# Small parts of weights: GpSimd's subtraction replaced by a negated copy on ScalarE and an accumulating DMA

## The chip, the cores and the metric

One core of a Trainium2 chip runs the program. The metric is the time of one execution in device microseconds (us). Engines are named as in the profile: PE (TensorE's products) and PEld (its weight loads), DVE (VectorE), ACT (ScalarE), POOL (GpSimd), SP (SyncE, which issues the loads).

## The reference

256 tokens of width 1024 go through two models one after the other, each of two layers and a final norm, in fp32. In a layer of the first ("block 1"):

```python
h = rmsnorm(x, norm_g)
proj = h @ w_in                       # split into 15 parts of four groups
y_a = conformer_conv(a_u, a_v, ...)   # 31 taps along the tokens, layernorm, silu
y_b = short_gated_conv(b_b, b_c, b_x, conv_b_w)
y_c = window_gqa(c_q, c_k, c_v, swa_sink)
y_d = neighborhood_attn(d_q, d_k, d_v, na_rpb)
x = x + concat([y_a*silu(a_z), y_b*silu(b_z), y_c*silu(c_z), y_d*silu(d_z)]) @ w_out
```

In a layer of the second ("block 2"):

```python
x = x + 0.5 * (silu(h @ wg) * (h @ wu)) @ wd   # ffn1, D_FF = 2816
x = x + mixing(rmsnorm(x))                     # forgetting and dilated attention, gated recurrence
x = x + 0.5 * (silu(h @ wg) * (h @ wu)) @ wd   # ffn2
```

## The kernel before

**Precision.** TensorE's fast format (fp32r) keeps fewer bits than fp32. So every weight w and every activation is split: hi = w rounded to fp32r, lo = w - hi. A product is made of three: hi by hi, hi by lo and lo by hi (`MM3`, `MMW`, `MM3n`).

**The weight stream.** All weights come from DRAM once, as 206 chunks in the order of their use, nearly all [128, 2048] fp32 (1 MB, sixteen 128x128 blocks). `weight_loads` asks for a tile `st` (3 buffers of them) and issues the load on SP. `weight_splits` takes chunk after chunk: it asks for a tile `hi` and a tile `lo` (3 buffers each) and works in halves [128, 1024]. For each half ACT copies st into hi, rounding, and then lo = st - hi is made on DVE or, for a share of the halves, on POOL: `share` is added up in `owed`, and each time it reaches 1 the half goes to POOL (`way = self.G`). The share is 0.6 in block 1 (`SHARE_A`), 0.25 in the feed-forward (`SHARE_F`) and 0.45 in the mixing of block 2 (`SHARE_B`); the first three chunks (`FAST`) never use POOL. After the last half st is free for the next load. `take` hands a chunk to the products, `drop` frees its hi and lo.

**Stages.** Two layers of block 1 (`mix_a`; the 31 taps of its convolution are 62 DVE instructions on the tile `ca`, from `hp`, in `a_u`); then twice feed-forward (`ffn`), mixing, feed-forward. In `ffn` the gate's sums leave the banks by `fg`, the up projection's by `fh`; `fs` is the gate after silu, `ha` the hidden operand.

**Order.** Each stage is a set of tasks (generators). `Scheduler.step` picks the instruction that can start first by its own estimates, less a priority; nothing but the order of instructions on each engine follows from them, and the waits are put in for the data. All helpers record their instructions at one line per kind: L470 is every ACT instruction, L493 every DVE and POOL one, L585 every DMA on SP, L574, L575 and L577 the products of `MMW`, L561 to L563 those of `MM3`.

Of the kernel before, what the change touches and what calls it, by code (L numbers as in the profile page):

```python
# [9 lines left out]
F32 = mybir.dt.float32  # L10
# [3 lines left out]
AF = mybir.ActivationFunctionType  # L14
# [4 lines left out]
T = 256  # L19
# [28 lines left out]
def out_order(nk, late):  # L48
    """(feature tile, k) of an output projection; the first tiles take the late k in a second sweep."""
    if not late:  # L50
        return [(fo, i) for fo in range(KT) for i in range(nk)]
    return ([(fo, i) for fo in range(OPEN) for i in range(nk - late)] +
            [(fo, i) for fo in range(OPEN) for i in range(nk - late, nk)] +
            [(fo, i) for fo in range(OPEN, KT) for i in range(nk)])
# [19 lines left out]
def weight_plan():  # L74
    """Chunks of the weight stream in the order of use: (key, source, layer, blocks);
    a block is (rows, columns) and lands as [128, len(columns)]."""
# [51 lines left out]
def const_arrays():  # L128
    """Tables that depend on the shapes alone."""
# [36 lines left out]
def param_columns(g):  # L166
    """Small parameters, features on partitions (layout only)."""
# [9 lines left out]
    for n in ("conv_a_w", "conv_b_w"):  # L177
# [26 lines left out]
FAST = 3  # L204
PARTS = {0: 4, 1: 4}
PRIO = dict(w1=0.8, w2=-1.8, w3=0.4, epilogue=0.5, gate=1.7, up=1.5, rstd=2.0, norm=1.3, values=0.7,
            conv=0.3, att=1.8, evac=1.1, level=0.3, prep=-0.7, rec=2.3, bias=-1.3, vg=0.2)
SHARE_F = 0.25
# [5 lines left out]
class Op:  # L214
    __slots__ = ("ways", "outs", "ins", "tset", "dep", "gen")

    def __init__(self, ways, outs, ins, tset=None):
        self.ways, self.outs, self.ins, self.tset = ways, outs, ins, tset
# [37 lines left out]
class Scheduler:  # L256
    """Orders the instructions of concurrent tasks (generators) by the estimated time at which each could start.
    Only the order follows from the estimates; every wait that the data needs is Tile's."""
# [20 lines left out]
    def advance(self, t):  # L279
        """Runs a task up to its next instruction, or until it has to wait."""  # L280
# [63 lines left out]
    def step(self):  # L344
# [41 lines left out]
        self.commit(op, eng, end)  # L386
# [11 lines left out]
class Builder:  # L398
# [104 lines left out]
    def VG(self, meth, out, *ins, **kw):  # L503
        """On the vector engine or, when that is done sooner, on GpSimd."""
        w, i = self._v("V", meth, out, ins, kw)
        w2, _ = self._v("G", meth, out, ins, kw)
        return Op([w, w2], [extent(out)], i)
# [28 lines left out]
    def MMs(self, products):  # L536
        """Products on distinct parts of the array, in one go: (out, lhsT, rhs, start, stop) each."""
# [16 lines left out]
    def MM3(self, out, ah, al, bh, bl, first, last):  # L554
        """Product of operands given as sums of two parts, less the product of the small parts."""
# [11 lines left out]
    def MMW(self, bank, wh, wl, x, first, last):  # L567
        """wh and wl against the parts x: [128, 2, 256], the bank's halves being the parts of the result."""
# [18 lines left out]

    def split(self, hi, lo, src):
# [21 lines left out]
    def weight_splits(self):  # L610
        for i in range(len(self.plan)):
# [5 lines left out]
            for j in range(parts):  # L617
# [5 lines left out]
                way = self.G if on_pool and i >= FAST else self.V  # L623
                yield way("tensor_tensor", lo[:, s], st[:, s], hi[:, s].bitcast(F32), op=ALU.subtract)
# [11 lines left out]
    def take(self, key):  # L636
        """The parts of the next chunk, its tiles, and the events of its pieces."""
# [12 lines left out]
    def dense_t(self, key, act, ready=None):  # L650
        """Features on partitions: a bank [128, nf, 256]."""
# [15 lines left out]
    def dense_w(self, key, act, ready):  # L667
        """Features on partitions: per feature tile a bank with the two parts of the result."""
# [13 lines left out]
    def dense_n(self, keys, act, width, ready=None):  # L682
        """Tokens on partitions: two banks, or halves of one, [128, width]."""
# [37 lines left out]
    def out_proj(self, key, act, nk, korder, late, coef, st, ready):  # L721
        """x += coef * act @ w, and the next norm's operands as the feature tiles finish."""
# [40 lines left out]
    def pair(self):  # L763
        """Operands of a product: large parts, small parts, and both side by side, [128, 8, 2, 256]."""
# [6 lines left out]
    def prep(self, st, fo):  # L771
        """x*g in two parts and the sums of squares, for feature tile fo."""
# [26 lines left out]
    def token_cols(self, tiles, out):  # L799
        """Sums over the partitions of [128, 256] tiles: [128 tokens, 2] in PSUM."""  # L800
# [10 lines left out]
    def bcast_cols(self, r, out):  # L811
        """[128 tokens, 2] to [128, 256] in PSUM, the same row on every partition."""
# [7 lines left out]
    def rstd(self, st, use):  # L820
        """st["r"]: [128 tokens, 2]; st["rbc"]: the same as rows, [128, 256], and what the phase asks for."""
# [131 lines left out]
    def heads(self, f, qT, kT, v, bias, nkeys, done, sink=None):  # L953
        """Heads 2f, 2f+1 (halves of feature tile f): qT(half, t), kT(half, n), v(kt, half), bias(half, t);
        done(bank) takes the bank with the outputs [128 (half, d), 256 queries]."""
# [62 lines left out]
    def rope(self, bank, ps, nf, cos, sin, o, tags):  # L1018
        """Rotary embedding of [128, nf, 256] with features on partitions, whose pairs lie 32 apart; o may hold the
        result."""  # L1020
# [14 lines left out]
    def mix_a(self, l, st, nxt):  # L1035
        nc, tc, s = self.nc, self.tc, self.s
        done = Event()
        with tc.tile_pool(name="mixa", bufs=1, reuse_waits="tile") as mp:
# [54 lines left out]
            def a_v(bank, ps):  # L1093
                """Raw like a_u: the norm's factor is applied here, to both."""
# [190 lines left out]
    def block_b_consts(self):  # L1285
        """Angles of the partial rotary embedding and the columns of the lower bounds."""
# [13 lines left out]
        # the angle over 2 pi modulo 1 with exact products: the angle in halves of 12 bits, 1 / 2 pi in three parts  # L1300
# [48 lines left out]
        # L = ln(max(lb, 1e-30)) in two steps that stay in the table's range  # L1349
# [11 lines left out]
    def mix_b(self, l, st, nxt):  # L1361
        nc, tc, s = self.nc, self.tc, self.s
        done = Event()
        with tc.tile_pool(name="mixb", bufs=1, reuse_waits="tile") as mp:
# [29 lines left out]
            def log1p_exp(ps, nch, cols=None):  # L1394
                """ln(1 + exp(-|z|)) for z and, given columns, for z + column."""
# [48 lines left out]
            def mixed(tl, m):  # L1444
                """Left halves of blocks of 2m from slot 0, right halves from slot 1."""
# [6 lines left out]
            def blocks(bank, t, left, right):  # L1452
                """left^T right within blocks of 64 tokens: [128 (block, s), (t, head), 64]."""
# [49 lines left out]
            def recurrence():  # L1503
                """A^T[s, t] of the gated recurrence: the diagonal, then pairs that meet in blocks of 2m tokens."""
# [120 lines left out]
            def dilated(f):  # L1625
                """One softmax over the keys of the three patterns, each key with its multiplicity."""
# [70 lines left out]
    def start(self, st):  # L1697
        """Loads, constants and the first norm's operands."""
# [35 lines left out]
    def warm(self):  # L1734
        """Keeps the tensor engine busy until the first operands are there, so that its clock is up by then."""
# [14 lines left out]
    def rescale(self, st, gf):  # L1750
        """x becomes the first block's output."""
# [136 lines left out]
```

## Time and profile before

| what | value |
|---|---|
| time, median of 3 runs | 1400.74 us (1397.69 to 1403.88) |
| profiled execution: span | 1401.3 us |
| PE busy | 1296.3 us (93%) |
| PEld busy | 1154.8 us (82%) |
| DVE busy | 1009.0 us (72%) |
| ACT busy | 776.4 us (55%) |
| POOL busy | 556.5 us (40%) |
| moved by DMA | 220.40 MB, 157 GB/s |

The page gives the profiled execution's time by its span alone; it is 0.6 us above the median. A busy share is a mean over stages that differ: what an engine's time is worth is read from the stage and from which wait ends last there. Busy times of PE are modelled.

### The profile page before, as it was taken

The page shows a single profiled execution, that of the slowest core. Times are in us where ns is not written, and L with a number is a line of the kernel's source. Part 1 is how long each engine was busy: PE and PEld are TensorE (multiplying, and loading weights), DVE is VectorE, ACT ScalarE, POOL GpSimd, SP SyncE. Part 2 cuts the span into 40 slices and gives each one's busy share as a digit, 9 for nine tenths or more (in the row PEclk, how much of TensorE's full clock was granted, in tenths as well). Part 3 has the DMA queues.
Part 4 walks back from the last instruction along what each step waited for, and adds up shares of the span by engine and source line. Part 5 has one row for each costly group of instructions (what it writes and reads, how often), then busy time and mean ns, then how long its engine had stood idle before and what let it go on. Part 6 is the DMA issues. An engine that isn't in the chain of part 4 may idle for free.

```text
span 1401.3 us, 21738 instructions
## 1 busy us (share of the span) xinstructions
PE 1296.3 (93%) x8530; PEld 1154.8 (82%) x8530; DVE 1009.0 (72%) x1478; ACT 776.4 (55%) x1277; POOL 556.5 (40%) x321
## 2 busy tenths in 40 slices
PE   8688996798989999889999999999999889999997
PEld 7677895787878789878788888888889778788886
DVE  7996789867997656778677656777656777677742
ACT  5444555355457547567555544556447667555542
POOL 5533662445324333553433323333333652433321
PEclk9888998899999999899999999999999989999999
DMA  7532543333536554323454554554554323455550
GB/s 261 188 120 72 156 157 120 120 121 120 185 122 213 202 185 151 132 80 121 158 200 183 188 203 155 204 182 181 192 191 156 126 83 127 151 182 196 193 181 31
DMA packets 39335, 220.40 MB, mean 157 GB/s; under 512 B 10176, under 2 KB 11968, under 8 KB 13760
## 3 DMA queue, kind: packets, MB, share of 16 engines
q1 hardware_dynamic: 39232, 219.01, 43.9%
q8 instruction: 67, 1.10, 0.3%
q14 instruction: 36, 0.29, 0.1%
HBM read 217.94 MB, written 1.05 MB: 156 GB/s over the span
## 4 chain that ended last, share of the span: by engine, by line
PE 62%; DVE 24%; ACT 6%; issue 5%; POOL 2%; DMA 0%; SPq 0%; DVEq 0%; POOLq 0%; ACTq 0%
PE bank L574 27%; PE bank L575 15%; DVE ca L493 6%; DVE lo L493 4%; PE bank L561 3%; PE bank L562 3%; PE bank L563 3%; PE bank L577 3%; DVE sp L493 3%; ACT hi L470 2%; PE bank L544 2%; DVE act L493 2%; PE bank L533 2%; DVE fh L493 2%; DVE x L493 1%
## 5 line engine op out<-in xcount | busy, mean ns | idle before, releaser
L493 POOL TENSOR_TENSOR lo<-st,hi 128x1024 fp32r<-128x1024 f32 (+1 forms) x142 | 354.5, 2499 | 483.4 <-ACT hi L470 481.2
L574 PE MATMUL bank<-act,hi 128*128 128x512 f32 x1456 | 524.5, 397 | 2.4 <-DVE act L493 2.3
L470 ACT ACTIVATE hi<-st 128x1024 fp32r<-128x1024 f32 (+3 forms) x416 | 428.2, 1035 | 90.3 <-PE bank L574 48.7
L575 PE MATMUL bank<-act,lo 128*128 128x256 f32 x1664 | 437.2, 283 | 5.0 <-DVE lo L493 4.2
L493 DVE TENSOR_TENSOR lo<-st,hi 128x1024 fp32r<-128x1024 f32 (+1 forms) x274 | 358.5, 1311 | 78.7 <-ACT hi L470 75.8
L575 PEld LDWEIGHTS bank<-act,lo 128*128 128x128 f32 x1664 | 315.6, 190 | 26.0 <-DVE lo L493 6.4
L574 PEld LDWEIGHTS bank<-act,hi 128*128 128x128 f32 x1456 | 276.2, 190 | 57.4 <-DVE act L493 3.6
L574 PE MATMUL bank<-ha,hi 128*128 128x512 f32 x672 | 238.1, 396 | 3.5 <-DVE ha L493 2.8
L561 PE MATMUL bank<-act,hi 128*128 128x256 f32 x720 | 214.7, 298 | 0.0
L562 PE MATMUL bank<-act,hi 128*128 128x256 f32 x720 | 205.7, 286 | 0.6 <-DVE act L493 0.6
L563 PE MATMUL bank<-act,lo 128*128 128x256 f32 x720 | 205.5, 285 | 0.0
L575 PE MATMUL bank<-ha,lo 128*128 128x256 f32 x704 | 193.3, 282 | 0.0
L574 PEld LDWEIGHTS bank<-ha,hi 128*128 128x128 f32 x672 | 126.8, 189 | 31.2 <-DVE ha L493 3.1
L561 PEld LDWEIGHTS bank<-act,hi 128*128 128x128 f32 x720 | 140.1, 195 | 6.4 <-issue 4.2
L562 PEld LDWEIGHTS bank<-act,hi 128*128 128x128 f32 x720 | 139.6, 194 | 1.1 <-DVE act L493 0.8
L563 PEld LDWEIGHTS bank<-act,lo 128*128 128x128 f32 x720 | 139.1, 193 | 0.0
L575 PEld LDWEIGHTS bank<-ha,lo 128*128 128x128 f32 x704 | 133.1, 189 | 2.8
L493 POOL TENSOR_TENSOR fs<-fs,rbc 128x512 f32<-128x512 f32 x44 | 62.0, 1410 | 114.5 <-ACT fs L470 108.0
L493 DVE SCALAR_TENSOR_TENSOR x<-bank,x 128x256 f32<-128x256 f32 x128 | 53.1, 420 | 68.7 <-PE bank L577 67.1
L493 POOL TENSOR_TENSOR sqa<-sqa,sq 128x256 f32<-128x256 f32 x60 | 54.1, 906 | 108.8 <-ACT sq L470 106.3
L577 PE MATMUL bank<-act,hi 128*128 128x512 f32 x208 | 83.1, 400 | 1.7 <-DVE act L493 1.7
L493 DVE SCALAR_TENSOR_TENSOR ca<-hp,cw,ca 128x256 f32<-128x256 f32 x120 | 81.1, 735 | 0.0
(218 smaller groups left out, 1601.4 us busy)
## 6 DMA issues: line engine op xcount, KB each, us to landing
st<-ws SPq DMA_DIRECT2D x197, 1024.0 KB, 4.8
st<-ws SPq DMA_DIRECT2D x2, 1040.0 KB, 4.8
st<-ws SPq DMA_DIRECT2D x4, 512.0 KB, 4.3
st<-ws SPq DMA_DIRECT2D x8, 192.0 KB, 5.2
nb<-rpb SPq DMA_DIRECT2D x16, 96.0 KB, 4.8
st<-ws SPq DMA_DIRECT2D x2, 768.0 KB, 4.3
out<-st SPq DMA_DIRECT2D x4, 256.0 KB, 2.8
cst<-cst SPq DMA_DIRECT2D x1, 832.5 KB, 8.7
```

Of the source, the lines that this page charges most:

```text
L470: return Op([("A", dur, lambda: self.nc.scalar.activation(out, in_, func, **kw))], outs, ins, ACT_SETS.get(func))
L493: return (eng, dur, lambda: fn(out, *ins, **kw)), [extent(a) for a in aps]
L533: return Op([("P", dur, lambda: self.nc.tensor.matmul(out, lhsT, rhs, start=start, stop=stop))], [extent(out)], [extent(lhsT), extent(rhs)])
L544: mm(o, l, r, start=st, stop=sp)
L561: mm(out, ah, bh, start=first, stop=False)
L562: mm(out, ah, bl, start=False, stop=False)
L563: mm(out, al, bh, start=False, stop=last)
L574: mm(out, wh, x, start=first, stop=False)
L575: mm(out[:, 0], wl, x[:, 0], start=False, stop=False)
L577: mm(out, wh, x, start=False, stop=True)
```

## The change

A half that fell to POOL is now made in two steps. ACT writes lo = -hi (a copy with scale -1), and then POOL issues a DMA that adds st to lo in place (`DMAadd`). POOL itself no longer works on the data. Which halves these are is decided by the same rule. The planner counts 1.2 us of POOL for an issue (`ADD_ISSUE`) and takes the result to be there 4.0 us later (`ADD_LATE`). Everything else of the diff removes comments.

```diff
+ADD_ISSUE = 1.2
+ADD_LATE = 4.0
...
-    def __init__(self, ways, outs, ins, tset=None):
-        self.ways, self.outs, self.ins, self.tset = ways, outs, ins, tset
+    def __init__(self, ways, outs, ins, tset=None, late=0.0):
+        self.ways, self.outs, self.ins, self.tset, self.late = ways, outs, ins, tset, late
...
-        self.commit(op, eng, end)
+        self.commit(op, eng, end + op.late)
...
+    def DMAadd(self, out, src):
+
+        return Op([("G", ADD_ISSUE, lambda: self.nc.gpsimd.dma_start(out, src, accum_op=ALU.add))],
+                  [extent(out)], [extent(src), extent(out)], late=ADD_LATE)
...
-                way = self.G if on_pool and i >= FAST else self.V
-                yield way("tensor_tensor", lo[:, s], st[:, s], hi[:, s].bitcast(F32), op=ALU.subtract)
+                if on_pool and i >= FAST:
+                    yield self.A(lo[:, s], hi[:, s].bitcast(F32), AF.Copy, scale=-1.0)
+                    yield self.DMAadd(lo[:, s].bitcast(F32), st[:, s])
+                else:
+                    yield self.tt(lo[:, s], st[:, s], hi[:, s].bitcast(F32), ALU.subtract)
```

There are 142 such halves before and 142 after. Since the planner's estimates change, it also orders other instructions differently.

**POOL in the first convolution.** lo_77, lo_78 and lo_79 are the three lo buffers. Before:

```order
L493 TENSOR_TENSOR lo_78<-st_73,hi_75 128x512
L493 TENSOR_TENSOR g_70<-par 128x8
L493 TENSOR_TENSOR lo_79<-st_71,hi_76 128x1024 x2
L493 TENSOR_TENSOR lo_77<-st_72,hi_74 128x1024
L493 TENSOR_TENSOR lo_78<-st_73,hi_75 128x1024
L493 TENSOR_TENSOR lo_79<-st_71,hi_76 128x1024
L493 TENSOR_TENSOR y_164<-oc,gz_162 128x256
L493 TENSOR_TENSOR lo_77<-st_72,hi_74 128x1024
```

After, in the same place (L592 is the issue of an accumulating DMA, L495 what L493 was):

```order
L592 DMA lo_78<-st_72 128x512
L592 DMA lo_79<-st_73 128x1024 x2
L592 DMA lo_77<-st_71 128x1024
L592 DMA lo_78<-st_72 128x1024
L592 DMA lo_79<-st_73 128x1024
L495 TENSOR_TENSOR y_164<-oc,gz_162 128x256 x2
L592 DMA lo_77<-st_71 128x1024
```

Each subtraction is an issue now, in the same sequence, and one more product of y stands on POOL.

**DVE in the first convolution.** ca is the convolution's sum, hp its padded input, cq and ck the queries and keys of the window attention that PE waits for. Before:

```order
L493 SCALAR_TENSOR_TENSOR ca<-hp,cw,ca 128x256 x6
L493 SCALAR_TENSOR_TENSOR gz_162<-th_159,bank_117 128x512
L493 SCALAR_TENSOR_TENSOR ca<-hp,cw,ca 128x256 x10
L493 TENSOR_TENSOR lo_77<-st_72,hi_74 128x1024
L493 TENSOR_TENSOR th_160<-bank_118,cst 128x512
L493 SCALAR_TENSOR_TENSOR ca<-hp,cw,ca 128x256
L493 TENSOR_TENSOR th_161<-th_161,cst 128x512
L493 TENSOR_TENSOR cq<-th_160,th_161 128x512
```

After:

```order
L495 SCALAR_TENSOR_TENSOR ca<-hp,cw,ca 128x256 x8
L495 SCALAR_TENSOR_TENSOR gz_162<-th_159,bank_117 128x512
L495 SCALAR_TENSOR_TENSOR ca<-hp,cw,ca 128x256 x9
L495 TENSOR_TENSOR lo_77<-st_71,hi_74 128x1024
L495 SCALAR_TENSOR_TENSOR ca<-hp,cw,ca 128x256
L495 TENSOR_TENSOR th_160<-bank_118,cst 128x512
L495 SCALAR_TENSOR_TENSOR ca<-hp,cw,ca 128x256
L495 TENSOR_TENSOR th_161<-th_161,cst 128x512
L495 TENSOR_TENSOR cq<-th_160,th_161 128x512
```

The order on DVE is nearly the same: a few taps stand on the other side of a neighbour.

**ACT in a feed-forward.** hi_74, hi_75 and hi_76 are the three hi buffers. Before:

```order
L470 ACTIVATE fs_5749<-fg_5746 128x512
L470 ACTIVATE fh_5751<-bank_120 128x256
L470 ACTIVATE hi_75<-st_73 128x1024
L470 ACTIVATE fh_5751<-bank_117 128x256
L470 ACTIVATE hi_75<-st_73 128x1024
L470 ACTIVATE ha<-fh_5751 128x2x256
L470 ACTIVATE fg_5745<-bank_119 128x256
```

After:

```order
L472 ACTIVATE fs_5825<-fg_5822 128x512
L472 ACTIVATE fh_5827<-bank_118 128x256
L472 ACTIVATE hi_76<-st_73 128x1024
L472 ACTIVATE lo_79<-hi_76 128x1024
L472 ACTIVATE fh_5827<-bank_122 128x256
L472 ACTIVATE hi_76<-st_73 128x1024
L472 ACTIVATE ha<-fh_5827 128x2x256
L472 ACTIVATE fg_5823<-bank_123 128x256
```

Once in two chunks a negated copy now stands between a chunk's first hi and the next copy out of a bank.

## Rows read from the trace of the kernel before

**Rows 1.** Page: busy us, share, count; then the chain that ended last, by engine

```profile
PE 1296.3 (93%) x8530; PEld 1154.8 (82%) x8530; DVE 1009.0 (72%) x1478; ACT 776.4 (55%) x1277; POOL 556.5 (40%) x321
...
PE 62%; DVE 24%; ACT 6%; issue 5%; POOL 2%; DMA 0%; SPq 0%; DVEq 0%; POOLq 0%; ACTq 0%
```

**Rows 2.** Page, groups: busy us, mean ns | idle before, what ended it

```profile
L493 POOL TENSOR_TENSOR lo<-st,hi 128x1024 fp32r<-128x1024 f32 (+1 forms) x142 | 354.5, 2499 | 483.4 <-ACT hi L470 481.2
```

**Rows 3.** Stretches, all instructions: length, PE, PEld, DVE, ACT, POOL busy, PEclk, DMA, GB/s

```profile
34.00:103.00 69.00, 50.03 (x392) 46.44 (x390) 67.83 (x112) 31.25 (x57) 32.33 (x15) 0.88 0.47 159
194.00:262.00 68.00, 52.77 (x403) 49.33 (x402) 63.89 (x118) 29.42 (x56) 26.67 (x13) 0.87 0.38 139
...
262.00:460.00 198.00, 184.70 (x1075) 158.64 (x1074) 161.11 (x257) 114.01 (x194) 81.59 (x49) 0.97 0.42 150
...
700.00:1050.00 350.00, 348.42 (x2007) 305.70 (x2006) 236.38 (x287) 190.25 (x277) 116.22 (x65) 1.00 0.52 188
```

**Rows 4.** Stretches, instructions on lo alone: length, PE, PEld, DVE, POOL busy

```profile
34.00:103.00 69.00, 32.45 (x115) 21.67 (x114) 10.17 (x7) 29.91 (x12) 0.88 0.47 159
194.00:262.00 68.00, 32.27 (x115) 21.98 (x114) 6.76 (x6) 24.06 (x10) 0.87 0.38 139
700.00:1050.00 350.00, 263.53 (x995) 186.93 (x995) 123.44 (x94) 75.69 (x31) 1.00 0.52 188
```

**Rows 5.** Instructions on ca: a tap's ns (least/middle/most); stretches (PE, PEld, DVE, ACT)

```profile
L493 DVE SCALAR_TENSOR_TENSOR ca<-hp,cw,ca x120: 468/473/2631, 42.2 to 254.8; 128x256 f32<-128x256 f32 x120
...
34.00:103.00 69.00, 0.00 (x0) 0.00 (x0) 43.08 (x61) 0.00 (x0) 0.88 0.47 159
194.00:262.00 68.00, 2.27 (x4) 1.05 (x4) 43.85 (x63) 0.63 (x1) 0.87 0.38 139
```

**Rows 6.** Timeline of DVE and POOL, 50 to 64 us: start, us, instruction, count

```profile
49.68 1.66 DVE L493 SCALAR_TENSOR_TENSOR ca<-hp,cw,ca 128x256 f32<-128x256 f32 x4
...
51.86 11.91 DVE L493 SCALAR_TENSOR_TENSOR ca<-hp,cw,ca 128x256 f32<-128x256 f32 x10
...
50.66 5.49 POOL L493 TENSOR_TENSOR lo<-st,hi 128x1024 fp32r<-128x1024 f32 x2 [4.61 <-ACT hi L470]
56.69 2.34 POOL L493 TENSOR_TENSOR lo<-st,hi 128x1024 fp32r<-128x1024 f32 x1 [0.54 <-ACT hi L470]
```

**Rows 7.** Waits of PE, 34 to 110, then 194 to 265 us: total, times, longest

```profile
PE bank L544 <- DVE ck L493: 12.0, 1, 12.0
PE bank L533 <- DVE ca L493: 4.7, 1, 4.7
...
PE bank L544 <- DVE ck L493: 11.2, 1, 11.2
PE bank L533 <- DVE ca L493: 4.0, 1, 4.0
```

**Rows 8.** Timeline of ACT and POOL in a feed-forward, 718 to 734 us

```profile
719.98 1.05 ACT L470 ACTIVATE hi<-st 128x1024 fp32r<-128x1024 f32 x1
722.42 0.39 ACT L470 ACTIVATE fh<-bank 128x256 f32<-128x256 f32 x1 [1.39 <-PE bank L577]
...
718.27 2.42 POOL L493 TENSOR_TENSOR lo<-st,hi 128x1024 fp32r<-128x1024 f32 x1 [7.49 <-ACT hi L470]
...
729.44 2.42 POOL L493 TENSOR_TENSOR lo<-st,hi 128x1024 fp32r<-128x1024 f32 x1 [7.49 <-ACT hi L470]
```

**Rows 9.** Waits of PE, 0 to 60, then 340 to 470 us: total, times, longest

```profile
PE bank L716 <- DVE lo L493: 3.8, 5, 1.2
...
PE bank L575 <- DVE lo L493: 4.2, 5, 1.9
```

**Rows 10.** Page, DMA: SP's queue (packets, MB, share), and issues (KB, us to landing)

```profile
q1 hardware_dynamic: 39232, 219.01, 43.9%
...
st<-ws SPq DMA_DIRECT2D x197, 1024.0 KB, 4.8
...
st<-ws SPq DMA_DIRECT2D x4, 512.0 KB, 4.3
```

More of the change, by code (lines that the diff above doesn't have):

```diff
@@ L214 @@
 class Op:
-    __slots__ = ("ways", "outs", "ins", "tset", "dep", "gen")
-    def __init__(self, ways, outs, ins, tset=None):
-        self.ways, self.outs, self.ins, self.tset = ways, outs, ins, tset
+    __slots__ = ("ways", "outs", "ins", "tset", "dep", "gen", "late")
+    def __init__(self, ways, outs, ins, tset=None, late=0.0):
+        self.ways, self.outs, self.ins, self.tset, self.late = ways, outs, ins, tset, late
 class Event:
```

## The prediction

> **What bounds the kernel now.** I read the chain that ended last, then busy time by stretch, then what PE waits for in the stretches where it idles. The chain runs on PE for 62% of the span and on DVE for 24%, on POOL for 2% [rows 1]. So POOL's 354.5 us of subtractions (142 of 2.5 us) [rows 2] are nowhere the last thing in themselves, and taking them off POOL is worth nothing directly. What counts is what they do to DVE.
>
> By stretch the kernel splits in two [rows 3]. In the feed-forward (700 to 1050 us) PE is busy 348.42 of 350 us: nothing that shortens another engine helps there. In the two convolution stretches of block 1 (34 to 103 and 194 to 262 us) DVE is busy 67.83 of 69 and 63.89 of 68 us, and PE idles for 19.0 and 15.2 us, at a granted clock of 0.88 and 0.87. From 262 to 460 us PE idles 13.3 us of 198.
>
> In the convolution stretches the same DVE instruction, one tap on 128x256, takes 468 ns at least, 473 in the middle and 2631 at most [rows 5]. The timeline shows why: four taps from 49.68 us, with POOL idle before 50.66, take 1.66 us together (0.415 each); the next ten, from 51.86, take 11.91 us, while POOL runs subtractions from 50.66 (two, 5.49 us) and from 56.69 us (2.34) [rows 6]. A tap has two inputs in SBUF, and it is held until POOL's subtraction is over; that is how I read these rows, and the forecast rests on it.
>
> **Taken out: DVE's holding.** Taps take 43.08 us for 61 and 43.85 us for 63 in the two stretches [rows 5]; at 0.415 us each they would be 25.3 and 26.1, so 17.8 and 17.7 us are holding. Subtractions are 29.91 of POOL's 32.33 busy us in the first stretch and 24.06 of 26.67 in the second [rows 3, 4], that is 0.93 and 0.90; their part of the holding is 16.5 and 15.9 us, 32.4 together.
>
> How much of it comes out of the span is read from what PE waited for [rows 7]. First stretch: 12.0 us for ck, which stands behind the ten held taps on DVE (11.91 us instead of 10 x 0.415 = 4.2, so 7.7 less), and 4.7 us for ca, the end of the convolution, which comes 16.5 us sooner and is no longer waited for: 12.4 us. Second stretch: waits of 11.2 and 4.0 us; with the first stretch's ratio (12.4 of 16.5) of 15.9 that is 11.9, under the 15.2 that was waited. Together 24 us; PE then has 50.03 us of work in some 57, and becomes the next bound if more were taken. Ends: 12 (half, if ACT or PE is late instead) and 32.4 (all).
>
> From 262 to 460 us DVE is at 161.11 of 198 us and PE's idle time is 13.3 us [rows 3]; PE waits for DVE's own lo there, 4.2 us in five waits [rows 9]. Less holding shortens DVE there too, but the same stretch gets the later adds and more ACT work (below). I take 6 us of the 13.3; ends 0 and 13.
>
> In the feed-forward the holding that goes is worth nothing: PE hardly waits.
>
> **Put in: the negated copy.** It is an ACT instruction on as many elements as hi's, so 142 x about 1.05 us (one of hi in [rows 8]) = 149 us on an engine busy for 776.4 of 1401.3 us [rows 1]. In the convolution stretches ACT goes from 31.25 to 44 (12 more) and from 29.42 to 40 us (10 more) of 69 and 68 [rows 3, 4]: cover enough. In the feed-forward ACT waits 1.39 us for PE ahead of a bank's copy [rows 8], and a copy of 1.05 us fits into that once per two chunks (POOL's subtractions there start 11.17 us apart [rows 8]). The order shows it there, between a hi and an fh. Cost taken: 0; if that cover is gone, the bank is emptied up to 1.05 us later, which costs PE only where it has no free bank.
>
> **Put in: issue and landing.** No accumulating DMA is in this trace. Issue on POOL: SP's issues don't count as busy, so the floor is 0; the ceiling is the 2.5 us of the subtraction replaced. I take 1.2. Landing: 512 KB of weights land 4.3 us and 1024 KB 4.8 us after issue [rows 10]. The add reads source and destination, 1024 KB, so I take 4.8; ends 4.3 and 9.6 (twice the load). From hi's end to lo that is 1.05 + 1.2 + 4.8 = 7.1 us (ends 5.4 and 13.2) instead of 2.5: 4.6 us later.
>
> Who waits for that? In the feed-forward a chunk takes 5.6 us (11.17 / 2). With three lo buffers a half that PE frees is read again after three chunk times less half a chunk, 14.0 us. In it hi takes 1.05 and the rest may take 12.9 us; 7.1 fits. SP gets st back 4.6 us later as well, and its load of 4.8 us is early enough for the same reason: three st buffers, 16.8 us round. Where there is no lead the delay shows: PE waits for DVE's lo at the start (3.8 us in five waits) and near 340 to 460 us (4.2 us in five) [rows 9]. A late add pushes PE once, and then the following chunks have that much more lead, so I count one push of 4 us at the start; that of the second place is in the 6 of 13.3 above. The queue's transfers took 43.9% of 16 engines' span for 219.01 MB [rows 10], 615 us, or 1.5 us for 512 KB; an add is one to three times that, 142 of them 210 to 630 us, so 59 to 89% in all. The middle doesn't fill the engines.
>
> **A rule against this change.** What [rows 6] show of two-input instructions has a counterpart in the other direction, of which this trace shows nothing. The Trainium skill, "SBUF — State Buffer", section "SBUF: two separate sides", warns that a DMA issued from GpSimd has its descriptors written by GpSimd's own cores, and that VectorE in a 2-port mode keeps them from writing them; section "A bandwidth-pool intuition that's wrong (but worth ruling out)" gives an example that goes from about 620 to about 3100 ns. An estimate from that page is 2.5 us more per landing, and by it the sum would be 2.5 us more at the start, 1378; by the rows alone it is 1375.
>
> **The sum.** Profiled execution 1401.3 us (its span; the page gives no time outside it, and the median of the three runs is 0.6 below). -24 (convolutions) - 6 (262 to 460) + 4 (start) = -26: 1375.3, less 0.6 for the median: 1375.
>
> **Rivals.**
> 1. ACT gives it back. ACT is on 6% of the chain [rows 1]. If the 149 us are on the path in that share, 9 us are lost, and if the convolution yields only its lower end, 12, the sum is -12 - 0 + 4 + 9 = +1: about 1402. For it: at the block changes ACT and DVE alternate on the path. Against: ACT has over a third of its time free in every row of [rows 3].
> 2. The change doesn't free DVE: issuing an add occupies POOL up to 2.5 us and holds DVE as the subtraction did. Then the 24 and the 6 are not there and the start's 4 us are: 1405. Against: the add's data goes over the DMA engines, not through POOL. On that, the Trainium skill, the same page, "Who interferes with whom": a VectorE instruction with two SBUF inputs contends with a GpSimd instruction that reads SBUF, not with one that only writes; by that rule this rival falls. No row here shows it.
> 3. Slower: adds land late in the feed-forward. At the upper ends the path is 13.2 us, over the 12.9 that three buffers allow; it decides from there. With 1 us more for waits on ACT (the 1.39 of [rows 8]) each add is 1.3 us late. There are 31 in 350 us [rows 4], so some 62 in the 700 us that are like it: 80 us. With 10 us at each of the two places without lead, and 30 gained: 1401 + 80 + 20 - 30 = 1470; half of it, if PE catches up between two adds, 1435. For it: the engines would be near 89% busy. Against: both ends must be at their worst.
>
> **How the numbers follow.** Forecast (1355 to 1394): 0.66. Rival 1: 0.12, a quarter of it still below 1394. Rival 2: 0.09. Rival 3: 0.13. A measurement of this kernel can tell about 0.5%, 7 us, from no change: faster (under 1393.7) 0.69, within 0.18 (three quarters of rival 1 and rival 2), slower 0.13. The range goes from all the holding and all of the 13.3 us gone (1401 - 32 - 13 = 1355) to 1408, which takes in rivals 1 and 2 and leaves rival 3 out. The forecast's own range is 1355 to 1394.
>
> **What would show it.** The taps' largest time falls from 2631 ns towards 473, and their sum in the convolution stretches from 43 us towards 27. PE's waits for ck (12.0 and 11.2) fall to about 4. ACT's busy time grows by some 149 us and POOL's falls by some 354. Landing of the adds reads 4 to 6 us. The feed-forward keeps its 11.17 us for two chunks; if that grows, rival 3 is at work. If taps stay at 2 us beside POOL's issues, rival 2. If taps are short and the span is the same, rival 1, and PE's waits then name ACT. The prediction is wrong if holding is not POOL's doing, or if PE's order of work after the convolution waits for something else that is as late.

## The result and the profile after

The changed kernel takes 1362.36 us (median of 4 runs, 1359.77 to 1365.31) against 1399.38 us for the kernel before on the same chip (1397.69 to 1403.88, 4 runs): a ratio of 0.9724, 95% interval 0.9691 to 0.9758, 37.0 us less. The forecast was 1375 us with a range of 1355 to 1408 and faster as the likeliest sign. The time and the sign came out. The sum behind them did not: the term for the holding and the term for the adds are both several times too small, and they are of opposite sign, as the runs below show.

First the page of the kernel after, to be laid beside [rows 1, 2]: busy time and share, the chain that ended last by engine, then the issues of the adds on POOL and the negated copies on ACT, each with the idle time before it.

```profile
PE 1277.9 (94%) x8530; PEld 1144.4 (84%) x8530; DVE 865.0 (64%) x1481; ACT 921.3 (68%) x1420; POOL 320.1 (24%) x318
...
PE 70%; ACT 10%; DVE 7%; DMA 7%; issue 3%; POOL 2%; SPq 0%; POOLq 0%; DVEq 0%; ACTq 0%
...
L592 POOL DMA_DIRECT2D lo<-st x142 | 123.9, 873 | 652.2 <-ACT lo L472 524.1
...
L472 ACT ACTIVATE lo<-hi 128x1024 fp32r<-128x1024 f32 (+1 forms) x142 | 149.3, 1052 | 3.8
```

DVE has lost 144 busy us without losing work, and its share of the chain falls from 24% to 7%. In its place DMA, which had 0%, has 7%, and ACT 10% instead of 6%. The taps that took up to 2631 ns [rows 5] are all short now, also the 34 that overlap an issue on POOL in time, which take 489 ns at most (all taps, ns: least, middle, most):

```profile
L495 DVE SCALAR_TENSOR_TENSOR ca<-hp,cw,ca x120: 472/481/490, 43.6 to 235.5; 128x256 f32<-128x256 f32 x120
```

The DMA part of the page answers to [rows 10]: SP's queue and POOL's (packets, MB, share of 16 engines), then loads and adds (KB, median us from issue to landing).

```profile
q1 hardware_dynamic: 39232, 219.01, 45.3%
q0 software_dynamic: 20448, 73.69, 28.5%
...
st<-ws SPq DMA_DIRECT2D x197, 1024.0 KB, 5.0
lo<-st POOLq DMA_DIRECT2D x136, 512.0 KB, 5.7
```

28.5% of 1358.0 us over 142 adds is 2.73 us of all 16 engines for each. SP's queue needs 45.3% x 1358.0 / 219.01 = 2.81 us for a megabyte, or 1.46 us for the 0.519 MB of an add. So an add uses the engines 1.9 times as long as a load of the same size. Together the queues are at 74% over the whole span, but not evenly. What PE waits for until the 298th us (total, times, longest) shows where that is felt; the first fence is of the kernel before, the second of the kernel after.

```profile
PE bank L544 <- DVE ck L493: 23.2, 2, 12.0
PE bank L533 <- DVE ca L493: 8.7, 2, 4.7
```

```profile
PE bank L565 <- DMA lo<-st: 24.9, 6, 6.0
PE bank L726 <- DVE lo L495: 3.5, 4, 1.2
...
PE bank L546 <- DVE ck L495: 1.1, 1, 1.1
```

Of the two waits for ck one of 1.1 us is left, the two for ca [rows 7] are gone, and six waits for an add that has not landed are there instead, 24.9 us. All of PE's waits that these two lists name, these and smaller ones, come to 52.1 us before and 35.8 after. Yet the kernel is 37 us faster, so the waits of this stretch are only a part of it.

A better ruler is progress: when PE starts the n-th matmul that reads a small part (lo). Both kernels have the same 3248 of them. In block 1, which ends near the 513th, this is how far each kernel is ahead of the one before, in us (worked out from the traces; the other columns are experiments below):

| small part read | at, before | after | POOL adds | no adds | copy twice | all DVE | placed |
|---|---|---|---|---|---|---|---|
| 65th (start) | 39.8 | -16.6 | -3.3 | -1.2 | -14.1 | -0.1 | 0.3 |
| 257th | 157.1 | 13.2 | -0.1 | 27.4 | 5.1 | 2.6 | 17.9 |
| 513th (end of block 1) | 298.5 | 24.6 | -6.9 | 54.5 | 11.4 | 7.0 | 44.4 |
| 961st | 477.6 | 43.6 | -3.9 | 74.7 | 22.8 | 26.3 | 59.1 |
| last | 1390.9 | 43.0 | -21.8 | 76.8 | -4.2 | 40.6 | 65.6 |

Each column is one profiled execution against one of the kernel before, and such a pair can differ from the medians: the spans of before and after are 43.3 us apart, the medians 37.0, and the execution of "placed" took 1337.24 us, 9.1 under its median. Differences of some 6 us between columns, and more for "placed", say nothing.

So the profiled execution after loses 16.6 us at the start, has gained 24.6 at the end of block 1 and 43.6 by the 961st, in the first feed-forward. From there on it holds its place. Block 1 as a whole, from the start to the 513th small part, in each kernel (length, busy us of PE, PEld, DVE, ACT, POOL, then PEclk, the mean granted TensorE clock with 1.00 for the 2.4 GHz level, DMA share, GB/s): the kernel before, the kernel after, and the one without adds.

```profile
0.00:298.00 298.00, 245.77 (x1721) 225.71 (x1722) 246.24 (x428) 146.40 (x268) 138.26 (x96) 0.90 0.43 144
```

```profile
0.00:274.00 274.00, 238.80 (x1725) 221.62 (x1726) 185.60 (x428) 186.83 (x311) 72.25 (x96) 0.96 0.86 229
```

```profile
0.00:244.00 244.00, 232.22 (x1724) 215.20 (x1725) 183.43 (x428) 186.23 (x311) 38.65 (x54) 0.99 0.53 177
```

DVE falls from 246 to 186 us for the same 428 instructions, which is what the change is about. The DMA engines go from 0.43 to 0.86, which is its price. PE's idle time falls by 17.0 us (52.2 to 35.2), and its busy time for the same work by 7.0 (245.77 to 238.80), while the mean granted clock rises from 0.90 to 0.96 (more on that in the last section). The DMA share could have been worked out: 42 of the 142 adds lie in block 1, and 42 x 2.73 us in 274 are 0.42 of the engines, on top of the loads' 0.43 x 298 / 274 = 0.47.

From the 513th to the 961st small part it is much the same, 19.0 us in two halves (before, then after): PE's idle time falls from 12.3 to 0.7 us, and its busy time for the same 921 matmuls from 166.78 to 159.38.

```profile
298.50:477.60 179.10, 166.78 (x921) 142.28 (x920) 146.01 (x216) 101.48 (x164) 72.58 (x43) 0.97 0.47 167
...
273.90:434.00 160.10, 159.38 (x921) 139.59 (x920) 123.96 (x218) 118.99 (x180) 39.82 (x41) 1.00 0.80 239
```

### The profile page after: what moved, and what is told of

It reads as the page before. It is cut to its first block, busy times and chain, and to the rows that moved or that the text cites. A ratio compares the mean times of both kernels' runs of the same rounds, so it can differ in the third digit from the quotient of the medians.

```text
span 1358.0 us, 21863 instructions
## 1 busy us (share of the span) xinstructions
PE 1277.9 (94%) x8530; PEld 1144.4 (84%) x8530; DVE 865.0 (64%) x1481; ACT 921.3 (68%) x1420; POOL 320.1 (24%) x318
## 3 DMA queue, kind: packets, MB, share of 16 engines
q1 hardware_dynamic: 39232, 219.01, 45.3%
q0 software_dynamic: 20448, 73.69, 28.5%
HBM read 217.94 MB, written 1.05 MB: 161 GB/s over the span
## 4 chain that ended last, share of the span: by engine, by line
PE 70%; ACT 10%; DVE 7%; DMA 7%; issue 3%; POOL 2%; SPq 0%; POOLq 0%; DVEq 0%; ACTq 0%
PE bank L576 34%; PE bank L577 19%; PE bank L579 4%; DMA lo<-st 3%; DVE sp L495 3%; ACT hi L472 3%; DMA st<-ws 3%; PE bank L563 2%; PE bank L565 2%; PE bank L564 2%; ACT lev L472 2%; PE bank L535 2%; ACT lo L472 1%; PE bank L546 1%; ACT pt L472 1%
## 5 line engine op out<-in xcount | busy, mean ns | idle before, releaser
L495 DVE TENSOR_TENSOR lo<-st,hi 128x1024 fp32r<-128x1024 f32 (+1 forms) x274 | 338.0, 1237 | 133.5 <-ACT hi L472 130.1
L592 POOL DMA_DIRECT2D lo<-st x142 | 123.9, 873 | 652.2 <-ACT lo L472 524.1
L565 PE MATMUL bank<-act,lo 128*128 128x256 f32 x720 | 208.9, 290 | 24.9 <-DMA lo<-st 24.9
L472 ACT ACTIVATE lo<-hi 128x1024 fp32r<-128x1024 f32 (+1 forms) x142 | 149.3, 1052 | 3.8
L495 POOL TENSOR_TENSOR fs<-fs,rbc 128x512 f32<-128x512 f32 x44 | 64.0, 1456 | 179.4 <-ACT fs L472 179.4
L495 DVE SCALAR_TENSOR_TENSOR x<-bank,x 128x256 f32<-128x256 f32 x128 | 53.6, 422 | 58.6 <-PE bank L579 56.7
L495 DVE TENSOR_TENSOR fh<-bank,fh 128x256 f32<-128x256 f32 x88 | 37.1, 423 | 76.6 <-ACT fh L472 76.6
```

What stands on the lines that cost most here:

```text
L472: return Op([("A", dur, lambda: self.nc.scalar.activation(out, in_, func, **kw))], outs, ins, ACT_SETS.get(func))
L495: return (eng, dur, lambda: fn(out, *ins, **kw)), [extent(a) for a in aps]
L565: mm(out, al, bh, start=False, stop=last)
L592: return Op([("G", ADD_ISSUE, lambda: self.nc.gpsimd.dma_start(out, src, accum_op=ALU.add))], [extent(out)], [extent(src), extent(out)], l ...
```

## The experiments

A program's time is compared by its ratio to the kernel before, which ran beside it on the same chip (1397.9 to 1402.0 us). Where medians of different experiments are subtracted below, some 4 us are chips and chance. The first two experiments keep the changed kernel's order of instructions on PE, DVE and ACT; in the others the planner orders anew.

**Is it the holding? The same program, with the add on POOL.** The order, the negated copies and the places of the adds stay; POOL adds st to lo itself.

```
-  nc.gpsimd.dma_start(out, src, accum_op=ALU.add)
+  nc.gpsimd.tensor_tensor(out.bitcast(F32R), out, src, op=ALU.add)
```

> The changed kernel with one thing put back: in the place of each accumulating DMA, POOL itself adds st to lo (one instruction with two inputs in SBUF). The order of all instructions, the negated copies on ACT among them, is that of the changed kernel. Theory 'holding' (the gain is DVE no longer held by POOL's two-input instructions): taps of 1 us and more are back, DVE's busy time is near 1000 us instead of 865, and the time is 1390 to 1410 us. Rival 'order' (the gain is the planner's other order, or halves being ready at better times): the time stays at 1355 to 1370 us.

Measured: 1425.89 us, ratio 1.0187 (1.0163 to 1.0211). It is slower than both. The 142 POOL instructions take 2501 ns again, and the taps are held again:

```profile
L592 POOL TENSOR_TENSOR lo<-lo,st 128x1024 fp32r<-128x1024 f32 (+1 forms) x142 | 354.8, 2501 | 523.4 <-ACT lo L472 497.2
...
L495 DVE SCALAR_TENSOR_TENSOR ca<-hp,cw,ca x120: 467/473/2626, 43.7 to 258.8; 128x256 f32<-128x256 f32 x120
```

In block 1 DVE is as busy as in the kernel before, and block 1 is not shorter (columns as above):

```profile
0.00:305.00 305.00, 244.96 (x1721) 224.71 (x1722) 248.40 (x427) 185.03 (x309) 143.95 (x95) 0.92 0.42 141
```

So the gain is not the new order's: it comes with POOL's instruction gone, and the taps show DVE held by that instruction. The run says one more thing: with the same work on POOL as before, the new order and the 149 us of copies on ACT cost 26.5 us.

**What do the adds cost? None at all.**

```
-  lambda: self.nc.gpsimd.dma_start(out, src, accum_op=ALU.add)
+  lambda: None
```

> The changed kernel with the 142 accumulating DMAs left out, so that lo stays -hi there: that part of the computation is missing. All else, the order too, is that of the changed kernel. It prices issue, landing and traffic of the adds. Theory 'cheap adds' (they are hidden but for a few places): 1350 to 1360 us. Rival 'adds bind block 1' (PE's 24.9 us of waits for the adds and the 10.7 to 13.0 us pieces of the chain on them come out nearly whole): 1330 to 1342 us.

Measured: 1325.57 us, ratio 0.9469 (0.9444 to 0.9495), 36.8 us under the changed kernel. "Cheap adds" falls. By the table 29.9 of it (54.5 - 24.6) are lost in block 1.

These two runs make an account of the change in three steps: new order and copies +26.5, no add on POOL -100.3 (1425.89 to 1325.57), the adds by DMA +36.8; together -37.0, as they must be. The steps were measured in this sequence; in another their sizes may differ. The middle step is not the holding alone: with POOL's add its result's lateness and the time that st waits for it go too. PE's waits for POOL's lo are 4.7 us in the whole run with it, and ACT's for a load 14.4 against 7.1 us. Most of the step is the holding: in block 1 DVE is busy 65.0 us less (248.40 to 183.43) for the same instructions, and block 1 is 61.4 us shorter.

**Where? Only in block 1, and only outside it.** The first kernel keeps the adds for the chunks of w_in and w_out, which block 1 uses in both layers, and lets POOL subtract elsewhere; the second does the opposite.

```
-  if on_pool and i >= FAST:
+  if on_pool and i >= FAST and not (self.plan[i][1] in ("w_in", "w_out")):
+      yield self.G("tensor_tensor", lo[:, s], st[:, s], hi[:, s].bitcast(F32), op=ALU.subtract)
+  elif on_pool and i >= FAST:
```

> Accumulating DMAs for the weights of block 1 alone; the other halves that fell to POOL are subtracted on POOL as before. By the two traces block 1 ends 24.6 us sooner after the change and the stretch behind it, where the first feed-forward's weights are split beside the set-up of block 2, gives 19 more. Theory 'two places' (each gain is made where its own weights are split): 1370 to 1380 us. Rival 'carried on' (the second gain follows from the first): 1355 to 1365 us.

> The opposite: POOL subtracts in block 1 as before, and the weights of block 2 alone have accumulating DMAs. Theory 'two places': 1375 to 1385 us. Rival 'carried on' (the second gain follows from the first): 1395 to 1402 us.

Measured: 1379.36 us, ratio 0.9853 (0.9826 to 0.9880), for block 1 alone; 1383.76 us, ratio 0.9881 (0.9857 to 0.9904), outside it alone. Against 1399.34 that is -20.0 and -15.6, together -35.6 of the -37.0. The two places add up; one is not the consequence of the other. By progress too, the second kernel gains 5.3 us up to the 513th small part and 18.2 from there to the 961st, the first 23.9 and 2.2.

**What is it about the adds in block 1: the engines' time, st, or lo?** In two kernels the add of a block 1 chunk goes to one of three spare tiles. In the first it reads lo, so that no matmul and no load waits for it; in the second it reads st, so that the loads wait again and the matmuls do not.

```
-  self.DMAadd(lo[:, s].bitcast(F32), st[:, s])
+  self.add_elsewhere(lo[:, s].bitcast(F32))    (first)
+  self.add_elsewhere(st[:, s])                 (second)
```

> The changed kernel, but in the first mixing block of both layers the accumulating DMA of a chunk reads the negated copy and adds it into one of three spare tiles that nobody reads, so the transfers and their issues stay where they were while no matmul and no weight load waits for them; the small parts of those chunks stay minus the rounded weight, so st is left out of them. Without any adds the kernel took 1325.6 us, with them 1362.4, and by the lag of the small parts about 30 of these 37 us lie in the first mixing block. Theory 'traffic' (the DMA engines are 86 to 89% busy there, and the adds slow the weight loads by sharing the engines): the time stays near the changed kernel's, 1355 to 1364 us. Theory 'late' (what costs is that the small part lands 5.7 us after its issue and that st is given back to the loads only then): about 1362 - 30 = 1332 us, 1328 to 1340. A value between splits the 30 us.

> As the run with the adds of the first mixing block sent to spare tiles (1343.6 us), but these adds read st instead of lo: the transfers stay, st goes back to the weight loads only when the add has landed, and still no matmul waits for a late lo. The small parts of those chunks stay minus the rounded weight. The changed kernel is at 1362.4 us, so 19 us are to be placed. Theory 'late st' (the loads wait for st): near the changed kernel, 1356 to 1364 us. Theory 'late lo' (the matmuls wait for the small part): near 1344, 1340 to 1349 us.

Measured: 1343.6 us, ratio 0.9597 (0.9569 to 0.9626), and 1354.66 us, ratio 0.9689 (0.9671 to 0.9708). Both theories of each run miss: the truth lies between them. Of the 36.8 us between no adds and all adds, 18.0 come with transfers alone in block 1 (and the real adds elsewhere), 11.1 more when st is held until landing, and 7.7 more when PE waits for lo. The last step is not clear of noise: the intervals of the second kernel and of the changed one overlap (0.9671 to 0.9708, 0.9691 to 0.9758). By progress at the 513th small part the three steps are 12.2, 13.5 and 4.2 us. So both traffic and lateness cost, lateness rather more in block 1, and most of the lateness seems to be the loads', not PE's. Block 1 of the two (columns as above):

```profile
0.00:256.00 256.00, 235.75 (x1723) 219.34 (x1724) 187.06 (x428) 186.85 (x310) 77.33 (x102) 0.96 0.91 246
```

```profile
0.00:270.00 270.00, 238.75 (x1726) 221.43 (x1727) 184.07 (x429) 187.16 (x311) 78.69 (x101) 0.94 0.89 235
```

DVE and ACT do the same work in both, and the DMA engines are near 0.9 in both; what sets them 14 us apart is when st comes free, beside an order that is not quite the same: the planner is told of a late lo in the first kernel and not in the second, and places a few per cent of the instructions elsewhere. ACT's waits for a load's landing before and after, and what SP's loads wait for after, tell the same (total, times, longest):

```profile
ACT hi L470 <- DMA st<-ws: 10.0, 7, 3.5
...
ACT hi L472 <- DMA st<-ws: 39.2, 13, 9.8
...
SPq L587 <- DMA lo<-st: 1051.3, 128, 22.6
```

A load waits for st, st for the add, the add for the engines, and ACT, which rounds the next chunk, for the load. What stays open: the first kernel also holds lo until the spare add has read it, and these adds land in 9.7 us (median), so its 18.0 us are transfers with that, not transfers alone. A fourth st buffer, which would bear on the middle step, was not tried.

**Is a smaller share of adds better?** In block 1 the share of halves that fall to copy and add is 0.6. With 0.4 and 0.2 the rest is subtracted by DVE.

```
-SHARE_A = 0.6
+SHARE_A = 0.4    (0.2 in the second)
```

> The changed kernel with 0.4 in place of 0.6 as the share of halves that take the negated copy and the add in the first mixing block; the others are subtracted by the vector engine, which is 45 us busy of 61 in the convolution stretch. Theory 'adds cost' (each add in the first block costs about 30 us / its adds, by traffic or by lateness): a third of the adds there gone, some 10 us, 1350 to 1356 us. Theory 'vector engine bound' (the vector engine's halves come on the path as soon as it has more of them): no gain or a loss, 1360 to 1372 us.

> The same with 0.2: two thirds of the first block's adds gone. Theory 'adds cost': some 20 us below the changed kernel, 1338 to 1348 us. Theory 'vector engine bound': later than with 0.4, 1360 to 1380 us. A minimum between the two, with 0.4 below both 0.6 and 0.2, would say that both are at work.

Measured: 1361.81 us, ratio 0.9719 (0.9704 to 0.9735), with 126 adds, and 1361.42 us, ratio 0.9718 (0.9690 to 0.9745), with 111. Neither differs from the changed kernel: "adds cost" falls in the form in which it was put, that every add less is time won. That what an add less wins, DVE's subtraction in its place loses, is a reading: with 0.2 block 1 has DMA at 0.60 and DVE at 214.21 us instead of 0.86 and 185.60, and is as long (273 us).

**All halves on DVE.** The kernel before, without POOL's subtractions and without adds.

```
-  way = self.G if on_pool and i >= FAST else self.V
+  way = self.V
```

> The kernel before with all halves subtracted by the vector engine, none by GpSimd and no adds. Theory 'holding was all that GpSimd's subtractions cost' and the vector engine has room (865 us busy after, plus 142 x about 1.1 us = 1021 of some 1350): 1335 to 1360 us, as good as the change or better. Theory 'vector engine bound' (in the first block it has 52 to 60 us of work in 61): 1375 to 1410 us.

Measured: 1366.18 us, ratio 0.9747 (0.9725 to 0.9768). This edit of one line comes within a quarter of a per cent of the change (0.9747 against 0.9724), between the bounds of the two theories. Its block 1 (columns as above):

```profile
0.00:291.00 291.00, 249.37 (x1721) 224.31 (x1722) 228.26 (x469) 147.23 (x268) 37.57 (x55) 0.89 0.45 151
```

It is 291 us long, 17 more than after, with DMA back at 0.45 and DVE at 228 us. But by the table it is level with the kernel before at the start, where after is 16.6 behind, and from the 961st to the last it gains 14.3 us, where the change gains nothing. The two kernels lose in different places.

**Each where it costs less.** DVE subtracts in the start's chunks; in the second kernel below also from 19 to 27, the first part of layer 2's block 1. Adds stay where the taps run.

```
-  if on_pool and i >= FAST:
+  if on_pool and i >= 8:                          (from8)
+  if on_pool and (8 <= i < 19 or i >= 28):        (conv)
```

> The same, with the vector engine's subtractions in chunks 3 to 7 alone and the adds from chunk 8 on. Theory 'each where it costs less': it gets the start's 17 us or most of them, 1345 to 1356 us. Theory 'the same either way': 1358 to 1366 us.

> The changed kernel with the adds of the first mixing block kept only where the convolution's taps load the vector engine, that is for chunks 8 to 18 and from 28 on; the vector engine subtracts in chunks 3 to 7 and 19 to 27. By the small parts' lag the kernel with all halves on the vector engine is 23.9 us ahead of the first kernel at the 192nd small part, where the changed kernel is 6.9 ahead, and falls 21.3 back from the 192nd to the 256th, where the changed one gains 6.3. Theory 'each where it costs less' (adds cost where DMA engines and st are short, the vector engine costs where the taps run): 1340 to 1352 us. Theory 'the same either way' (both only move the wait; the share from 0.2 to 0.6 made no difference): 1358 to 1366 us.

Measured: 1358.98 us, ratio 0.9714 (0.9695 to 0.9734), and 1346.37 us, ratio 0.9626 (0.9610 to 0.9642). The first is no better than the change: the 16.7 us that it regains at the start (0.1 instead of -16.6 at the 65th) are 10.1 at the 513th and 1.5 at the last. The second is faster than both kernels; its interval lies below the change's. It is the column "placed" of the table. Its block 1:

```profile
0.00:254.00 254.00, 235.60 (x1723) 215.94 (x1724) 203.23 (x445) 171.65 (x294) 60.09 (x78) 0.98 0.75 216
```

With the same 126 adds as share 0.4 it is 15 us faster, so which chunks take the add counts here, more than how many. This is the execution that took 1337.24 us, so its block 1 may be some us shorter than usual. PE's waits for adds are down to a few us (total, times, longest; the whole span):

```profile
PE bank L565 <- DMA lo<-st: 3.6, 2, 3.1
PE bank L577 <- DMA lo<-st: 2.1, 3, 0.9
```

**Has ACT room? Each negated copy made twice.**

```
   yield self.A(lo[:, s], hi[:, s].bitcast(F32), AF.Copy, scale=-1.0)
+  yield self.A(lo[:, s], hi[:, s].bitcast(F32), AF.Copy, scale=-1.0)
```

> The changed kernel with each negated copy made twice into the same place before its add: 142 more scalar-engine copies of 1.05 us, 149 us more of that engine, and each add about 1.05 us later. Theory 'the scalar engine had room' (it is 68% busy, and waits for the weight loads in the first mixing block): 1362 to 1370 us, no more than the adds' being later by a microsecond would give. Theory 'the scalar engine's copies cost' (its copies pace the first mixing block as the adds do): a third of the 149 us or more is in the first block's 42 copies and on the path, 1375 us or more.

Measured: 1409.82 us, ratio 1.0074 (1.0051 to 1.0098). Another 150 us of ACT, in the order that the planner then makes, cost 47.5 us of the span and more than undo the change. That order differs in many places on DVE and ACT, and no run takes the two apart. PE's waits for adds nearly double, and ACT's copies rise on the chain (by line: ACT lo 4% instead of 1%):

```profile
L472 ACT ACTIVATE lo<-hi 128x1024 fp32r<-128x1024 f32 (+2 forms) x286 | 299.8, 1048 | 6.4
...
PE bank L565 <- DMA lo<-st: 46.5, 12, 8.2
```

"ACT had room" falls for the second copy in that order. In the two feed-forwards in the middle it costs nothing even so (at the 1409th and at the 2433rd small part it is 34.1 us behind the changed kernel); 13.2 us are lost in block 1, 7.6 from there to the 961st, 13.3 from the 961st to the 1409th, and 13.1 behind the 2433rd. What the first copy costs is not settled by this: the 26.5 us of the run with POOL's adds hold the first copies and the new order together.

## Why the prediction was right, and where only its sum was

**DVE's holding: the mechanism right, the size too small by far.** Taps fall from at most 2631 to at most 490 ns, and the run with POOL's adds brings them back. The two terms for it, -24 and -6, are 30 us; taken away at the new order, with the rest of POOL's adds, it is worth 100.3. Two things in the working failed. It limited the gain to the part of PE's waits that named ck and ca, and it called 32.4 us all the holding there is: those were the taps in two stretches. Other DVE instructions were held as well, all over block 1: DVE's 428 there took 246.24 us and take 185.60, 60.6 less, where the taps' own holding was 35.5 by the prediction's count. And PE did the same work in less time at a higher mean clock, which no term had. The waits shown for PE were less than what the holding cost, and it took them for the measure.

**From 262 to 460 us, -6.** Measured, from the 513th to the 961st small part: 43.6 - 24.6 = 19.0 us, above the end of 13 that was given. The prediction read PE's idle time of 13.3 us [rows 3] as all there was to get, and set later adds against half of it. Of idle time 11.6 us came out, nearly all of it, and PE's waits for a late small part are absent there in the kernel after; the other 7.4 are PE's busy time.

**The negated copies at 0.** Their duration was right, 142 x 1052 ns = 149.3 us. In the feed-forward behind the first mixing the 0 holds even for two copies. In block 1 the ground for it is not safe: "cover enough" was read from ACT's busy share, and there the same work once more, in another order, cost 13.2 us. What the first copies cost is at most the 26.5 us of copies and order together, unless the new order by itself gained.

**Issue and landing.** Issue: 0.87 us, under the 1.2 taken. It counts as busy, 123.9 us in all, so POOL's busy time fell by 236 us and not by the 354 that the prediction's signs name. Landing: 5.7 us in the middle and at most 13.0 over the span; from 100 to 300 us it is longer (from issue to landing, that window):

```profile
DMA to landing us min/median/max: 4.0/7.1/12.0
```

The 4.8 taken was too short and the end of 9.6 too low for the worst. In the same window SP's loads land later too (the kernel before, then after):

```profile
st<-ws SPq DMA_DIRECT2D x20, 1024.0 KB, 4.8
...
st<-ws SPq DMA_DIRECT2D x24, 1024.0 KB, 6.4
```

So the longer landing is not the adds' own; the DMA engines are at 0.86 to 0.89 in the convolution stretches of block 1 (34 to 95 and 180 to 250 us). The rule against this change is that of the Trainium skill, "SBUF — State Buffer", section "SBUF: two separate sides". No run here shows descriptors held back by VectorE: an issue took 846 to 1037 ns wherever it stood, and the landing was 0.9 us over the 4.8 assumed, not the 2.5 of that estimate; but no run was made to test it.

**The push of 4 us at the start.** It was 16.6, and it was not the only one. The step that failed is "the middle doesn't fill the engines": the forecast of 59 to 89% for the whole span holds (74%), but block 1 alone runs at 0.86, and st comes back late there. Its price is 36.8 us in all, 29.9 of them in block 1. The chain of the kernel after shows the links, each a landing (start us, us, what):

```profile
38.09 12.97 DMA lo<-st
...
148.57 9.13 DMA lo<-st
157.84 7.60 DMA st<-ws
170.53 10.72 DMA lo<-st
...
190.12 7.15 DMA st<-ws
199.82 9.30 DMA lo<-st
```

Before, DMA had 0% of the chain. The prediction's 59 to 89% were worked out from the queue's 43.9%, an average over stages, though the share of halves that fall to the adds is 0.6 in block 1 and 0.25 in the feed-forward.

**The rivals.** Rival 1 (ACT gives it back) is not the outcome, but a part of it may be true: 26.5 us were lost to copies and order together. Rival 2 (an issue holds DVE) is out: the taps beside issues take 489 ns at most. By the Trainium skill, "SBUF — State Buffer", section "Who interferes with whom", it falls, and the trace agrees. Rival 3 (late adds in the feed-forward) is out: from the 1473rd to the 1857th small part, all in one feed-forward, PE takes 133.9 us in both kernels, and the adds there land in 8.3 us at most, so that hi's end to lo is about 1.05 + 8.3 = 9.4 us, under the 12.9 from which it decides. What it described happened in block 1, where there is no such lead.

**What hit the time.** The forecast came near 1362 by terms that offset, which is luck: 70 us too little for the holding (100.3 against 30), 33 too little for the adds (36.8 against 4), 26.5 too little for copies and order. The errors sum to 70.3 - 32.8 - 26.5 = 11 us below the forecast, against 1375 - 1362.4 = 12.6 measured; the rest is the kernel before, 1399.4 beside the changed kernel and 1400.7 in the runs shown ahead of the prediction. (The 0.6 us taken off at the end of the sum compared a span with a time; for the kernel after the profiled execution's time is 1.8 us above its span.)

PE's own account adds to that. The forecast's -26 was worked out from PE's idle time, and between the two profiled executions that fell by 24.9 us net, from 105.0 to 80.1. PE's busy time for the same 8530 matmuls fell by 18.4 more, from 1296.3 [rows 1] to 1277.9, at a mean granted clock of 0.959 and 0.978. For that the sum had no term.

## What to carry to other kernels

A wait that names an engine is only the last link: to price what slows that engine, look also at the busy time of all its instructions in the stage against their unheld time, not only at the waits of another engine. Moving work to DMA engines that are idle on average costs what they are short of in the stage where the work lands, and a transfer that keeps a load's buffer until it lands costs the next load too. Where two places for a piece of work cost the same overall, look where along the span each loses: putting each half where its engine had room gave 16 us more than the change, with fewer adds.

## What the runs showed of the hardware

- An accumulating DMA from SBUF to SBUF of 512 KB took 0.87 us of POOL to issue, 5.7 us to land, and 2.73 us of the 16 DMA engines, 1.9 times what a load of as many bytes took in the same run.
- POOL's instruction with two SBUF inputs held DVE's in two forms, lo = st - hi (taps to 2631 ns) and lo = lo + st (to 2626 ns). In the feed-forward the holding cost nothing: in the run with POOL's adds PE was busy 349.80 of 350 us (700 to 1050 us), with DVE at 240.57.
- TensorE's busy time for the same work went with its granted clock. Block 1 has the same matmuls in every kernel, to a few that the trace lacks: PE was busy 249.37 us there at a mean granted clock of 0.89 (all halves on DVE), 245.77 at 0.90 (before), 238.80 at 0.96 (after) and 232.22 at 0.99 (no adds), where 1.00 is the 2.4 GHz level and the mean mixes in stretches at 1.2 GHz. Of the 54 us by which the kernel without adds is ahead at the end of block 1, 13.5 are that. In most of these runs the clock was higher where PE idled less in block 1 (52.2, 35.2 and 11.8 us in the last three), but not in all: it was 0.89 with 41.6 us idle (all halves on DVE) and 0.92 with 60.0 (POOL's adds), so how much PE idles does not settle it alone.
